# The second part of 76 split weight tiles: made by ScalarE and an adding DMA from GpSimd where VectorE subtracted

## The chip, the cores and the metric

The kernel runs on one core of one Trainium2 chip. The metric is the device time of one execution in microseconds (us). Times given as median are over three runs.

## What is computed

The reference is a network of two layers over 1024 tokens of width 1024, in float32. The first layer mixes tokens by attention in a sliding window, the second by the HGRN2 recurrence. Each mixer is followed by an MLP that squares a ReLU between two matrix products of width 4096.

```python
for layer in range(DEPTH):
    h = rmsnorm(x, mix_norm[layer])
    y = sliding_window_attention(h, ...) if layer % N_MIXERS == 0 else hgrn2_recurrence(h, ...)
    x = x + y
    h = rmsnorm(x, mlp_norm[layer])
    x = x + jnp.square(jax.nn.relu(h @ w_up[layer])) @ w_down[layer]
return rmsnorm(x, final_norm)
```

## The kernel before

**Split products.** A float32 matrix product is made of three products in the faster type float32r. Each operand is split in two parts: the first part, `hi`, is the operand rounded to float32r, and the second part, `lo`, is what is left of it. The three products are hi x hi, hi x lo and lo x hi (`mm3`, line 392), all added up in PSUM. For a weight tile of 128 x 512 this is done by `weight_split` (line 410): a cast writes `hi` into a buffer `wh`, and a subtraction writes `lo` into a buffer `wl`. There are five buffers each of `wr` (the raw tile as it is loaded), `wh` and `wl` (line 41). The cast may be given to ScalarE or VectorE; the subtraction goes to VectorE.

**Fewer products.** Large products run by a scheme of Strassen's kind. `strassen_weights` (line 590) loads four weight tiles `a[i, k]`, makes four sums of them, `s1` to `s4`, and gives up to seven tiles to be split, numbered 1 to 7. Of these, three are loaded tiles and not sums: `a[0, 0]` is number 1, `a[0, 1]` number 2 and `a[1, 1]` number 4. `done` names the tiles that are left out. `inner` brings in further tiles, of a second step of the scheme on smaller blocks; their names are pairs such as `(2, "12")`, and some of them are loaded tiles too.

Two functions call it:

- `pair` (line 711) is one of 16 steps of the first matrix product of an MLP, for m = 0 to 15. For m = 0 and 1 the tiles 1 and 2 are done already, so of the loaded ones number 4 is split. From m = 2 on, the tiles 2, 3 and 4 are left to inner products, so number 1 is split, and it is the first in the order.
- `two` (line 1282) is one of two units for each of the eight heads of HGRN, 16 units in all. In the first head the tiles 1 and 2 are done already; in the other 14 units all seven tiles are split.

A product of a tile is four times three matmuls of 128 x 128 by 128 x 512 (`product`, line 584): in each three, two use `wh` and the third uses `wl`. Inner products work on 256 columns.

**The order of the work.** The kernel doesn't issue its operations as they are written. `Schedule` (line 142) takes all of them with their costs, what they read and write and which engines may run them. It plays them through with these costs and latencies and issues them in the order that comes out, engine by engine (`order`, line 185). Each engine's queue, and SP's queue of DMAs, then runs in that order, and each instruction waits for what it needs. A buffer is given to the next tile when its last reader has finished. Operations on weights get a lead of 100 places (`LEAD`, line 136). A change of one cost or engine can therefore move operations elsewhere. Line 334 stands for nearly every instruction in the profile, because a helper records them there, so instructions are told apart by their tiles: `wr`, `wh`, `wl` as above, `p` and `q` for PSUM, `a`, `t` and `m` for the other buffers on the chip, `d` for DRAM.

Of the kernel before, what the change touches and what calls it, by code (L numbers as in the profile page):

```python
# [10 lines left out]
F32 = mybir.dt.float32  # L11
F32R = mybir.dt.float32r
I32 = mybir.dt.int32
AF = mybir.ActivationFunctionType
ALU = mybir.AluOpType
# [7 lines left out]
TH = T // NH  # L23
# [256 lines left out]
class Net:  # L280
# [126 lines left out]
        self.dma(r, src, 4 * P * TH)  # L407
        return r

    def weight_split(self, z):  # L410
        hi, lo = (self.tile(tag, BUFS[tag], (P, TH), F32R) for tag in ("wh", "wl"))
        self.copy(hi, z, TH, ("ACT", "DVE"), False)
        self.tt("any", lo, z, hi.bitcast(F32), ALU.subtract)
        return hi, lo

    def weight(self, src):

        self.s.lead = LEAD
        w = [self.weight_split(self.raw(src[:, c : c + TH])) for c in (0, TH)]
        self.s.lead = 0  # L420
        return w
# [168 lines left out]
    def strassen_weights(self, first, second, done=(), inner=()):  # L590

        self.s.lead = LEAD
        a = {(i, k): self.raw(src[:, k * TH : k * TH + TH]) for i, src in enumerate((first, second)) for k in range(2)}
        s1, s2, s3, s4 = (self.t(tag="m") for _ in range(4))
        self.tt("any", s1, a[1, 0], a[1, 1], ALU.add)  # L600
        self.tt("any", s2, s1, a[0, 0], ALU.subtract)
        self.tt("any", s3, a[0, 0], a[1, 0], ALU.subtract)
        self.tt("any", s4, a[0, 1], s2, ALU.subtract)
        order = [(1, a[0, 0]), (5, s1), (2, a[0, 1]), (6, s2), (3, s4), (7, s3), (4, a[1, 1])]
        order = [(name, z) for name, z in order if name not in done]
        own = {2: a[0, 1], 3: s4}
        for leaf, rows, names, places in inner:
            if rows:
                up, low = (z if isinstance(z, View) else own[z] if isinstance(z, int) else self.raw(z) for z in rows)
                upper, lower = self.t(tag="m"), self.t(tag="m")  # L610
                L, R = slice(0, 2 * P), slice(2 * P, TH)
                self.tt("any", upper[:, L], low[:, L], low[:, R], ALU.add, 2 * P)
                self.tt("any", upper[:, R], upper[:, L], up[:, L], ALU.subtract, 2 * P)
                self.tt("any", lower[:, L], up[:, L], low[:, L], ALU.subtract, 2 * P)
                self.tt("any", lower[:, R], up[:, R], upper[:, R], ALU.subtract, 2 * P)
                self.rows[leaf] = {"12": up, "56": upper, "73": lower, "4": low}
            for name, place in zip(names, places):
                order.insert(place, ((leaf, name), self.rows[leaf][name]))
        self.fourth = s4
        w = {name: self.weight_split(z) for name, z in order}  # L620
        self.s.lead = 0
        return w

# [1021 lines left out]
```

## Time and profile before

| | |
|---|---|
| median of three runs | 2114.9 us (2114.53 to 2116.04) |
| the profiled execution, span from the first to the last instruction | 2113.4 us; a time of its own beside the span isn't listed |
| granted TensorE clock, mean | 0.998 |
| DMA queue of SP | 225664 packets, 405.16 MB, 57.1% of 16 engines' span |
| packets of GpSimd's own DMAs | none |

In order of time the program does the attention layer (to about 300 us), the first MLP (its 16 pairs to about 620, its second product to about 920), HGRN (to about 1470, its projections in the first two thirds of it), and the second MLP (its 16 pairs from about 1480 to 1765, then its second product and the output).

The profile tells of engines by short names: PE is TensorE's matmuls, PEld its loads of weights (which overlap PE), DVE is VectorE, ACT ScalarE, POOL GpSimd, SP SyncE. The ends of matmuls are modelled, so a busy PE is not a PE at its peak. A row of a group gives the engine, the operation, out<-in by buffer names, the shape and the count, then busy us and the mean ns of one, then the idle time of the engine just before. A row of a timeline gives the start in us, the duration, the engine and the operation; in brackets, how long the engine sat idle before it and what ended that. SPq is the sequencer that issues SP's DMAs.

### The profile page before, as it was taken

The numbers are of one execution on the slowest core, as the hardware profiler recorded it, in microseconds if no ns is written. First come the engines' busy times: TensorE is split into PE (matmuls) and PEld (weight loads), VectorE is DVE, ScalarE is ACT, GpSimd is POOL, SyncE is SP. The second block draws the span as 40 slices with busy tenths as digits, with TensorE's granted clock in tenths as the row PEclk, the third lists the DMA queues.
The fourth block names the chain that finished last, engine by engine and source line by source line (L and its number), as shares of the span: only waits on it lengthen the run. The fifth ranks groups of instructions, "written<-read, shape, count | busy, mean of one in ns | idle before, by whom it ended". The sixth has DMA issues, their size and how long they took to land.

```text
span 2113.4 us, 35648 instructions
## 1 busy us (share of the span) xinstructions
PE 2090.4 (99%) x12220; PEld 1738.6 (82%) x12220; DVE 1900.2 (90%) x3922; ACT 1121.3 (53%) x2284; POOL 62.3 (3%) x121
## 2 busy tenths in 40 slices
PE   9999999999999999999999999999999999999998
PEld 7778777888888888888888888888788888888887
DVE  8889899999998989999888888888999999998995
ACT  5557777656564323556444444453765556432453
POOL 4030000000000000000000000000000000000000
PEclk9999999999999999999999999999999999999999
DMA  6212277867678967632222222566786767896632
GB/s 209 82 51 79 87 235 258 289 227 245 230 243 281 318 215 256 222 125 76 101 100 96 96 100 90 201 234 219 274 271 231 242 225 251 287 318 217 232 119 80
DMA packets 225845, 407.43 MB, mean 193 GB/s; under 512 B 25344, under 2 KB 30464, under 8 KB 225664
## 3 DMA queue, kind: packets, MB, share of 16 engines
q1 hardware_dynamic: 225664, 405.16, 57.1%
q8 instruction: 96, 1.57, 0.3%
q14 instruction: 85, 0.70, 0.1%
HBM read 321.17 MB, written 83.89 MB: 192 GB/s over the span
## 4 chain that ended last, share of the span: by engine, by line
PE 84%; DVE 8%; ACT 3%; issue 2%; DMA 1%; POOL 0%; POOLq 0%; SPq 0%; ACTq 0%; DVEq 0%
PE p L334 43%; PE q L334 41%; DVE t L334 4%; DVE a L334 2%; ACT t L334 2%; DVE m L334 1%; DVE wl L334 1%; ACT a L334 1%; DMA d<-t 1%; DMA t<-d 1%; ACT m L334 0%; DMA a<-in_x 0%; ACT wh L334 0%; DVE wh L334 0%; DMA wr<-in_wqkv 0%
## 5 line engine op out<-in xcount | busy, mean ns | idle before, releaser
L334 PE MATMUL p<-a,wh 128*128 128x512 f32 (+1 forms) x2880 | 816.1, 367 | 0.7 <-DVE t L334 0.4
L334 PE MATMUL q<-a,wh 128*128 128x512 f32 x2112 | 661.3, 394 | 1.2 <-ACT t L334 1.0
L334 PEld LDWEIGHTS p<-a,wh 128*128 128x128 f32 x2880 | 513.3, 188 | 93.9 <-DVE a L334 0.8
L334 PE MATMUL p<-a,wl 128*128 128x512 f32 (+1 forms) x1440 | 523.9, 364 | 0.1
L334 PEld LDWEIGHTS q<-a,wh 128*128 128x128 f32 x2112 | 389.0, 188 | 85.0 <-ACT t L334 1.9
L334 PE MATMUL q<-a,wl 128*128 128x512 f32 x1056 | 415.0, 393 | 1.1 <-DVE wl L334 1.1
L334 PEld LDWEIGHTS p<-a,wl 128*128 128x128 f32 x1440 | 270.7, 188 | 44.6 <-DVE wl L334 0.9
L334 DVE TENSOR_TENSOR wl<-wr,wh 128x512 fp32r<-128x512 f32 x352 | 240.6, 685 | 7.2 <-ACT wh L334 1.3
L334 DVE TENSOR_TENSOR wl<-m,wh 128x512 fp32r<-128x512 f32 x338 | 230.1, 686 | 10.3 <-ACT wh L334 0.9
L334 PEld LDWEIGHTS q<-a,wl 128*128 128x128 f32 x1056 | 198.3, 188 | 47.4 <-DVE wl L334 1.5
L334 ACT ACTIVATE t<-t 128x512 f32<-128x512 f32 x268 | 168.9, 633 | 121.7 <-DVE t L334 116.2
L334 ACT CAST wh<-wr 128x512 fp32r<-128x512 f32 x249 | 154.1, 619 | 147.9 <-PE p L334 104.0
L334 DVE TENSOR_TENSOR t<-t,t 128x512 f32<-128x512 f32 (+3 forms) x337 | 197.3, 598 | 16.9 <-DMA t<-d 10.2
L334 ACT CAST a<-t 128x512 fp32r<-128x512 f32 (+1 forms) x216 | 130.1, 611 | 146.3 <-PE q L334 83.0
L334 DVE TENSOR_TENSOR a<-t,a 128x512 fp32r<-128x512 f32 (+2 forms) x314 | 205.6, 676 | 2.0 <-ACT a L334 1.7
L334 ACT CAST wh<-m 128x512 fp32r<-128x512 f32 x231 | 143.4, 621 | 118.1 <-PE p L334 49.0
L334 ACT COPY t<-q 128x512 f32<-128x512 f32 (+2 forms) x201 | 112.2, 560 | 102.3 <-PE q L334 89.7
L334 DVE TENSOR_TENSOR m<-wr,wr 128x512 f32<-128x512 f32 (+1 forms) x188 | 120.9, 645 | 13.4 <-DMA wr<-in_down 13.0
L334 PE MATMUL p<-wh,a 128*128 128x512 f32 x384 | 127.1, 402 | 1.0 <-DVE c L334 1.0
L334 DVE TENSOR_TENSOR t<-t,p 128x256 f32<-128x256 f32 x294 | 117.6, 413 | 0.3
L334 PEld LDWEIGHTS q<-t,t 128*64 128x64 f32 (+1 forms) x2160 | 95.5, 144 | 13.9 <-issue 7.8
L334 PE MATMUL q<-t,t 128*64 128x32 f32 (+2 forms) x2160 | 105.4, 229 | 0.0
(129 smaller groups left out, 2393.7 us busy)
## 6 DMA issues: line engine op xcount, KB each, us to landing
t<-d SPq DMA_DIRECT2D x548, 256.0 KB, 4.0
d<-t SPq DMA_DIRECT2D x244, 256.0 KB, 2.8
wr<-in_down SPq DMA_DIRECT2D x224, 256.0 KB, 4.1
wr<-in_up SPq DMA_DIRECT2D x178, 256.0 KB, 3.8
wr<-in_win SPq DMA_DIRECT2D x68, 256.0 KB, 2.6
a<-d SPq DMA_DIRECT2D x60, 256.0 KB, 4.8
wr<-in_wqkv SPq DMA_DIRECT2D x48, 256.0 KB, 2.6
d<-a SPq DMA_DIRECT2D x48, 256.0 KB, 3.9
```

What stands on the lines that cost most here:

```text
L334: fn(*[place(a) for a in args], **{k: place(v) for k, v in kw.items()})
```

## The change

Where a tile to be split is one of the four that `strassen_weights` loads, and its name is a number and not a pair, the split is done another way. The cast to `wh` is bound to ScalarE. ScalarE then writes the negative of `wh` into `wl`, and a DMA that GpSimd issues adds the raw tile to `wl` where it lies. To the planner, the DMA costs 1100 ns on GpSimd and 3000 ns more until it has landed. Sums, inner tiles and every weight tile that doesn't come by way of `strassen_weights` are split as before.

```diff
-    def weight_split(self, z):
+    def weight_split(self, z, by_dma=False):
         hi, lo = (self.tile(tag, BUFS[tag], (P, TH), F32R) for tag in ("wh", "wl"))
+        if by_dma:
+            self.copy(hi, z, TH, ("ACT",), False)
+            self.act(lo, hi.bitcast(F32), AF.Copy, scale=-1.0)
+            self.add_by_dma(lo.bitcast(F32), z)
+            return hi, lo
         self.copy(hi, z, TH, ("ACT", "DVE"), False)
         self.tt("any", lo, z, hi.bitcast(F32), ALU.subtract)
         return hi, lo
+
+    def add_by_dma(self, out, in_):
+        self.op("Pool", self.nc.gpsimd.dma_start, [out], [out, in_], 1100.0, out, in_, accum_op=ALU.add, tail=3000.0)
...
-        w = {name: self.weight_split(z) for name, z in order}
+        loaded = set(a.values())
+        w = {name: self.weight_split(z, z in loaded and not isinstance(name, tuple)) for name, z in order}
```

## The prediction

> **What bounds the kernel now.** I read the page first: busy time of each engine, then the busy time by stage, then the order of instructions around the tiles that the change touches.
>
> ```profile
> span 2113.4 us, 35648 instructions
> PE 2090.4 (99%) x12220; PEld 1738.6 (82%) x12220; DVE 1900.2 (90%) x3922; ACT 1121.3 (53%) x2284; POOL 62.3 (3%) x121
> ```
>
> TensorE (PE) is busy 99% of the span and VectorE (DVE) 90%. An average over stages doesn't say which of them sets the pace where the change acts, so the next view cuts the span into stretches: length, then busy time of PE, PEld, DVE, ACT and POOL, the granted clock, the share of the DMA engines.
>
> ```profile
> 390.00:620.00 230.00, 230.00 (x1382) 204.10 (x1381) 212.95 (x450) 134.58 (x225) 0.00 (x0) 1.00 0.73 240
> 920.00:960.00 40.00, 39.64 (x179) 31.89 (x179) 35.42 (x64) 20.31 (x38) 0.00 (x0) 1.00 0.23 82
> 960.00:1060.00 100.00, 98.97 (x780) 81.39 (x779) 91.99 (x205) 48.91 (x105) 4.63 (x4) 1.00 0.27 93
> 1060.00:1370.00 310.00, 308.55 (x2601) 254.06 (x2600) 270.70 (x614) 141.96 (x309) 3.68 (x12) 1.00 0.33 113
> 1370.00:1470.00 100.00, 99.25 (x679) 81.97 (x678) 80.78 (x175) 40.90 (x82) 0.57 (x2) 1.00 0.68 225
> 1500.00:1545.00 45.00, 42.89 (x199) 34.49 (x198) 44.66 (x98) 27.12 (x52) 0.00 (x0) 1.00 0.80 275
> 1545.00:1765.00 220.00, 220.00 (x1317) 195.03 (x1317) 204.74 (x434) 130.69 (x220) 0.00 (x0) 1.00 0.73 241
> ```
>
> 390 to 620 and 1545 to 1765 are the pairs of the two MLP layers: PE is busy in all 230.00 and all 220.00 us, at a granted clock of 1.00. 920 to 1470 is HGRN: PE idles 0.36 + 1.03 + 1.45 + 0.75 = 3.59 us. 1500 to 1545 is the start of the second MLP, where DVE is busy in 44.66 of 45 us and PE idles 2.11. All that a faster VectorE can give back lies in these 3.59 + 2.11 = 5.7 us. Nothing else of VectorE's time is on the path: PE bounds the kernel.
>
> **The change part by part.** By the code, 76 tiles take the new way: one a pair in the MLP (2 layers x 16 = 32), and in HGRN one in each of the first two units and three in each of the other 14 (44).
>
> ```profile
> L334 DVE TENSOR_TENSOR wl<-wr,wh 128x512 fp32r<-128x512 f32 x352 | 240.6, 685 | 7.2 <-ACT wh L334 1.3
> L334 ACT ACTIVATE t<-t 128x512 f32<-128x512 f32 x268 | 168.9, 633 | 121.7 <-DVE t L334 116.2
> ```
>
> VectorE loses 76 x 0.685 = 52.1 us of subtractions; ScalarE gains 76 negative copies at 0.633 = 48.1 us, and the casts of these tiles that the planner used to give to VectorE (19 of the 76, by the listing of both programs; 9 other casts go the other way). VectorE had 17 us free in 390 to 620, ScalarE 95. Since PE is full there, the 52 us are hidden already and give nothing. PE's order of work in the listing stays the same but for a few neighbours swapped at the third and fourth pairs and in HGRN, so what counts is whether the second part (wl) is there when PE loads it. Here is one such tile, that of m = 8 in the first MLP (timeline: start, duration, engine, operation):
>
> ```profile
> 464.72 0.62 ACT L334 CAST wh<-wr 128x512 fp32r<-128x512 f32 x1 [0.73 <-PE p L334]
> ...
> 465.98 0.68 DVE L334 TENSOR_TENSOR wl<-wr,wh 128x512 fp32r<-128x512 f32 x1
> ...
> 466.69 0.33 SPq L334 DMA_DIRECT2D wr<-in_up  x1
> ...
> 470.40 1.30 ACT L334 ACTIVATE t<-t 128x512 f32<-128x512 f32 x2
> ...
> 471.20 0.19 PEld L334 LDWEIGHTS q<-a,wl 128*128 128x128 f32 x1
> ```
>
> The cast waits until PE frees a wh buffer and ends at 465.34. Two dependent ScalarE instructions take 1.30, so the negative copy ends 0.65 later, at 465.99. A handover costs about 0.03: the subtraction ends at 466.66, and the load that waited for it issues at 466.69. PE loads wl at 471.20. So the new DMA may take, from issue to landing, 471.20 - 465.99 - 0.06 = 5.15 us. I call that time L. The same distance at the last even pair (m = 14, second MLP), at an odd pair (m = 9; two casts in the line, the second ends at 482.20), at m = 4 of the second MLP, at m = 2 there, and at the HGRN tile with the shortest distance:
>
> ```profile
> 1733.27 0.62 ACT L334 CAST wh<-wr 128x512 fp32r<-128x512 f32 x1 [0.72 <-PE p L334]
> ...
> 1739.76 0.19 PEld L334 LDWEIGHTS q<-a,wl 128*128 128x128 f32 x1
> ```
> ```profile
> 480.86 1.34 ACT L334 CAST wh<-wr 128x512 fp32r<-128x512 f32 x2 [0.42 <-PE p L334]
> ...
> 489.43 0.19 PEld L334 LDWEIGHTS q<-a,wl 128*128 128x128 f32 x1
> ```
> ```profile
> 1548.33 0.60 ACT L334 CAST wh<-wr 128x512 fp32r<-128x512 f32 x1
> ...
> 1554.09 0.19 PEld L334 LDWEIGHTS q<-a,wl 128*128 128x128 f32 x1
> ```
> ```profile
> 1512.51 0.62 ACT L334 CAST wh<-wr 128x512 fp32r<-128x512 f32 x1
> ...
> 1519.54 0.19 PEld L334 LDWEIGHTS q<-a,wl 128*128 128x128 f32 x1
> ```
> ```profile
> 994.34 0.63 ACT L334 CAST wh<-wr 128x512 fp32r<-128x512 f32 x1
> ...
> 1005.91 0.19 PEld L334 LDWEIGHTS p<-a,wl 128*128 128x128 f32 x1
> ```
>
> Less 0.65 and 0.06 each: 5.16 for the ten even pairs from m = 6 on; 6.5 for the twelve odd ones from m = 5; 4.45 for the two of m = 4; 5.7 for m = 2 and 3 (four tiles, all put at the shortest); over 10 in HGRN, whose 44 tiles are safe, as are those of m = 0 and 1.
>
> What L will be, the trace doesn't show: no DMA is issued from GpSimd and none adds. The nearest rows are the issues in 390 to 620 (KB, median us to landing), one of quiet HGRN (1060 to 1370), the queue's share of 16 engines in 390 to 620, and the smallest regular GpSimd operation:
>
> ```profile
> q1 hardware_dynamic: 30109, 54.84, 72.2%
> ...
> wr<-in_up SPq DMA_DIRECT2D x62, 256.0 KB, 3.6
> d<-t SPq DMA_DIRECT2D x50, 256.0 KB, 3.0
> ```
> ```profile
> d<-t SPq DMA_DIRECT2D x44, 256.0 KB, 2.0
> ```
> ```profile
> L334 POOL TENSOR_SCALAR m<-c 128x4 f32<-128x4 f32 x32 | 12.8, 407 | 174.3 <-PE q L334 130.8 <-DVE a L334 18.7 <-DVE m L334 9.6
> ```
>
> A packet costs 0.722 x 16 x 230 / 30109 = 88 ns. A tile is 128 packets of 2 KB, 8 an engine, 0.7 us; the sum has to read the destination as well, so one more 0.7. Low end: as quick as a quiet store, 2.0. High end: a store's time and a load's one after the other, plus a GpSimd start, 3.0 + 3.6 + 0.4 = 7.0. I take 3.6 + 0.7 + 0.4 = 4.7, a load of this stage with a second read and a GpSimd start, because the traffic around it is the same. The Trainium skill, "DMA: Bandwidth & Descriptors", section "Anatomy of one DMA", fits DMAs issued from GpSimd by 2.0 us plus bytes over 436e3; for 256 KB that is an estimate of 2.6 us, and by it even m = 4 would not wait. No run here shows it yet.
>
> At L = 4.7 only m = 4 is late, twice 4.7 - 4.45 = 0.25: +0.5 us. One wait goes:
>
> ```profile
> 1523.70 0.62 ACT L334 CAST wh<-wr 128x512 fp32r<-128x512 f32 x1 [0.77 <-PE q L334]
> ```
> ```profile
> 1533.43 0.51 PE L334 MATMUL q<-a,wl 128*128 128x512 f32 x1 [1.08 <-DVE wl L334]
> ```
>
> At m = 3 of the second MLP the cast was done at 1524.32, but the subtraction stood in VectorE's queue and PE waited 1.08 us. By DMA the tile lands near 1524.32 + 0.65 + 0.06 + 4.7 = 1529.7, in time: -1.1 us.
>
> The DMA also holds the raw tile (wr) longer. In the first example its buffer is free at about 465.34 + 0.65 + 0.06 + 4.7 = 470.75 instead of 466.66, so SP, whose queue is in order, issues the next wr load 4.1 us later, and everything behind it waits. After an odd pair:
>
> ```profile
> 447.27 1.62 SPq L334 DMA_DIRECT2D wr<-in_up  x2
> ```
> ```profile
> 454.64 0.68 DVE L334 TENSOR_TENSOR m<-wr,wr 128x512 f32<-128x512 f32 x1
> ```
>
> The load issued at 447.27 would move about 3.3 later, to 450.6, and land at 454.2 with 3.6: still ahead of the sum that reads it at 454.64. The listing puts the neighbouring load ahead of it. If L is longer, VectorE waits first, and its sums are needed by PE some us later; I cost this at nothing, the cover being those 0.4 us and VectorE's lead. GpSimd's queue has 76 more instructions and nothing urgent behind them.
>
> Sum on the profiled execution: 2113.4 + 0.5 - 1.1 = 2112.8. Its own time isn't listed; the median of the runs is 2114.9, 1.5 above the span, and I add that: 2114.3.
>
> **The rivals.** (a) The DMA becomes what PE waits for. The delay repeats at every pair, because each cast waits for PE anew, and costs 10 x (L - 5.15) + 2 x (L - 4.45) + 4 x (L - 5.7) + 12 x (L - 6.5) - 1.1, each bracket from zero up. It passes 0.2% of the time (4.2 us, about what a measurement of this kernel can tell from no change) at L = 5.5, where it is 3.5 + 2.1 - 1.1 = 4.5. At 7.0 it is 18.5 + 5.1 + 5.2 + 6.0 - 1.1 = 33.7, so 2149; halfway, at 6.25, 11.0 + 3.6 + 2.2 - 1.1 = 15.7, so 2131. For it: the margin is 0.4 us on an operation that the trace doesn't hold, with DMA engines 73% busy. Against it: SP stands waiting for this very landing, so little new traffic starts beside it.
>
> One thing could lengthen L from VectorE's side:
>
> ```profile
> L334 DVE CAST wh<-m 128x512 fp32r<-128x512 f32 x26 | 11.1, 425 | 9.1 <-PE q L334 8.9
> ```
>
> These casts run at 425 ns where subtractions of the same size take 685. The Trainium skill, "SBUF — State Buffer", section "Who interferes with whom", says that such a fast copy locks GpSimd out of a shared port while a DMA's descriptors are to be written, and that a two-operand subtraction doesn't. By it, a DMA that meets a cast is up to 0.43 us late: L = 5.13, 2 x 0.68 - 1.1 = +0.3 us, still no measurable change.
>
> (b) Faster by more than 0.2%: the relief of VectorE and the new order empty all 5.7 us of PE's idle time in the changed stages: 2109.2. For it, DVE is full in 1500 to 1545; against it, HGRN's waits are short ones at each change of operand, and ScalarE, which serves many of them, gets more work.
>
> (c) ScalarE's added copies delay PSUM reads in HGRN. One 0.65 us in each of the 16 units makes 10.4 us, so about 2125. Against it: ScalarE is busy 141.96 of 310 us there, and in the listing no added copy stands directly ahead of the reads that PE waits for.
>
> **How the numbers follow.** Forecast (L below 5.5) 0.55; (a) 0.35, little of it past its end; (b) 0.05; (c) 0.05. The range goes from 2111, the edge of 0.2%, to 2149, the bound of (a); some 1 in 10 is left out. Faster 0.05, same 0.55, slower 0.35 + 0.05 = 0.40.
>
> **What would show it.** Right: PE busy in all of 390 to 620 again, GpSimd's DMAs landing in 4 to 5.3 us, no PE wait on wl at m = 3, and VectorE some 50 us less busy at nearly the same span. Wrong: waits of PE on a DMA of wl from wr at each pair (a), or on t in each HGRN unit (c). If VectorE's relief moved the span by more than 5.7 us, my reading of PE as the bound would be wrong.

## The result, and the profile after

| | before | changed |
|---|---|---|
| median of four runs each, on the same chip | 2114.7 us (2113.38 to 2116.04) | 2132.9 us (2129.43 to 2134.91) |
| profiled execution: span | 2113.4 us | 2131.3 us (its own time 2133.1) |

The ratio is 1.0081, 95% interval 1.0068 to 1.0094: the change costs some 17 us. The page of the changed kernel:

```profile
span 2131.3 us, 35981 instructions
PE 2097.2 (98%) x12220; PEld 1739.9 (82%) x12220; DVE 1857.3 (87%) x3844; ACT 1172.5 (55%) x2364; POOL 126.9 (6%) x197
```

VectorE has lost 42.9 us of work (1900.2 to 1857.3), ScalarE has gained 51.2, and the span, with the same 12220 matmuls, is 17.9 us longer. So work came off an engine that PE hardly waited for. The same seven stretches as in the prediction (length, busy time of PE, PEld, DVE, ACT and POOL, granted clock, DMA share, GB/s):

```profile
390.00:620.00 230.00, 227.35 (x1358) 200.46 (x1358) 202.70 (x432) 137.60 (x229) 10.35 (x12) 1.00 0.80 245
920.00:960.00 40.00, 40.00 (x182) 32.56 (x180) 35.36 (x68) 17.19 (x32) 0.88 (x1) 1.00 0.34 112
960.00:1060.00 100.00, 96.47 (x704) 78.41 (x704) 81.94 (x184) 59.81 (x121) 13.27 (x14) 0.98 0.42 113
1060.00:1370.00 310.00, 307.29 (x2636) 253.09 (x2635) 247.17 (x566) 165.36 (x351) 32.12 (x45) 1.00 0.49 133
1370.00:1470.00 100.00, 98.89 (x695) 82.05 (x694) 80.66 (x181) 41.12 (x83) 0.57 (x2) 1.00 0.73 240
1500.00:1545.00 45.00, 42.00 (x177) 33.19 (x176) 39.68 (x83) 30.75 (x58) 3.62 (x4) 0.96 0.83 257
1545.00:1765.00 220.00, 216.58 (x1276) 190.12 (x1275) 195.43 (x414) 133.83 (x224) 9.48 (x11) 0.99 0.79 249
```

PE was busy in all of 390 to 620 and 1545 to 1765; now it idles 2.65 and 3.42 us there. And the clock column, 1.00 throughout before, shows 0.98, 0.96 and 0.99 in three rows: some matmuls ran slowly. Matching the matmuls of the two traces one by one tells where the delay grows: 4.1 us in the first MLP, most of it at 375 to 425; 4.5 at 950 to 1000, where HGRN begins; 8.8 at 1525 to 1600, the first pairs of the second MLP. Elsewhere it changes by less than 1 us in all, and the last matmul ends 17.0 us later.

**PE waits for the new DMA, but not at each pair.** The DMA's rows (duration of the issue on GpSimd; then who waited, us and times; then issue to landing):

```profile
L334 POOL DMA_DIRECT2D wl<-wr x76: 859/862/1037, 338.5 to 1769.2; - x76
...
who waited for it (us, times):
  PEld q L334: 9.5, 8
  PE q L334: 6.3, 3
...
DMA to landing us min/median/max: 3.2/4.5/7.7
```

The median landing, 4.5 us, is what the prediction took (4.7). But only three tiles stopped the matmuls, for 6.3 us. The same query in five stretches, in order of time: m = 3 to 5 of the first MLP, m = 6 to 15, HGRN from 1000 us on, m = 2 to 5 of the second MLP, and m = 6 to 15:

```profile
L334 POOL DMA_DIRECT2D wl<-wr x3: 862/862/862, 369.1 to 411.2; - x3
DMA to landing us min/median/max: 5.6/6.4/7.1
```
```profile
L334 POOL DMA_DIRECT2D wl<-wr x10: 859/862/864, 431.5 to 598.1; - x10
DMA to landing us min/median/max: 4.0/4.9/6.4
```
```profile
L334 POOL DMA_DIRECT2D wl<-wr x40: 859/862/887, 1002.3 to 1358.3; - x40
DMA to landing us min/median/max: 3.2/3.4/7.6
```
```profile
L334 POOL DMA_DIRECT2D wl<-wr x4: 862/862/1009, 1523.1 to 1581.6; - x4
DMA to landing us min/median/max: 4.9/6.5/7.7
```
```profile
L334 POOL DMA_DIRECT2D wl<-wr x10: 859/862/864, 1603.6 to 1769.2; - x10
DMA to landing us min/median/max: 3.7/5.2/6.1
```

These are medians of 3.4 us in quiet HGRN, 4.9 and 5.2 in the regular pairs (m = 6 to 15), and 6.4 and 6.5 in the pairs before them. Where the DMA engines are busier it takes longer: they are busy 0.47 of the time from 1000 to 1360, 0.80 from 430 to 630, 0.87 from 335 to 430, 0.82 from 1500 to 1600; the HGRN tile of 7.6 is issued at 1358, where the share has risen to 0.86. The late tiles are m = 4 of the first MLP (landing 7.1 us, PE waits 1.80), and m = 2 (7.7, 2.50) and m = 4 (6.6, 2.02) of the second. This is m = 2 there, in the timeline (start, duration; in brackets the idle time before and what ended it):

```profile
1521.51 0.62 ACT L334 CAST wh<-wr 128x512 fp32r<-128x512 f32 x1
...
1522.17 0.64 ACT L334 ACTIVATE wl<-wh 128x512 fp32r<-128x512 f32 x1
...
1523.10 1.01 POOL L334 DMA_DIRECT2D wl<-wr  x1 [3.64 <-PE q L334]
...
1530.86 0.50 PE L334 MATMUL q<-a,wl 128*128 128x512 f32 x1 [2.50 <-DMA wl<-wr]
```

Negative copy to 1522.80, GpSimd starts 0.29 us behind it, landing at 1530.81, and the matmul has waited 2.50 us.

**After a long wait the clock is halved for a while.** Windows of the changed kernel: just behind that wait, a little later, and behind the wait of 1.80 us at 398.9:

```profile
1532.00:1535.40 3.40, 3.40 (x10) 2.67 (x9) 3.40 (x8) 1.26 (x2) 0.00 (x0) 0.52 0.89 277
1535.50:1540.00 4.50, 4.50 (x21) 3.68 (x20) 4.50 (x10) 4.32 (x8) 0.86 (x1) 0.99 0.80 279
```
```profile
399.00:403.00 4.00, 4.00 (x24) 3.57 (x25) 0.80 (x3) 1.25 (x3) 0.00 (x0) 1.00 0.71 226
```

The matmuls fall 1.5 us further behind in these 3.4 us, on top of the 2.50; behind 1.80 us nothing of the kind. The same happens behind the waits of 2.02 us at m = 4 (clock 0.50 from 1569.7 to 1573.1) and 2.14 us at the entry of HGRN, below: 1.5 and 1.7 us, so 4.7 us in all.

**At the entry of HGRN the planner has moved a tanh.** ScalarE before, at the square root of HGRN's norm (ACTIVATE sm<-sm), and after, where the same root stands at 977.62:

```profile
972.22 0.20 ACT L334 ACTIVATE sm<-sm 128x4 f32<-128x4 f32 x1 [0.29 <-DVE sm L334]
972.44 1.28 ACT L334 ACT_TABLE_LOAD   x1
973.74 1.16 ACT L334 ACTIVATE t<-t 128x512 f32<-128x512 f32 x2
```
```profile
974.38 1.28 ACT L334 ACT_TABLE_LOAD   x1
975.67 0.63 ACT L334 ACTIVATE t<-t 128x512 f32<-128x512 f32 x1
976.32 1.28 ACT L334 ACT_TABLE_LOAD   x1
977.62 0.20 ACT L334 ACTIVATE sm<-sm 128x4 f32<-128x4 f32 x1
...
978.32 1.28 ACT L334 ACT_TABLE_LOAD   x1
979.61 0.63 ACT L334 ACTIVATE t<-t 128x512 f32<-128x512 f32 x1
```

One tanh now goes ahead of the root, so three table loads of 1.28 us stand where one stood. VectorE waits for the second tanh, PE for VectorE, and the half clock follows (window of the changed kernel, clock 0.50):

```profile
980.27 0.69 DVE L334 SCALAR_TENSOR_TENSOR t<-t,t 128x512 f32<-128x512 f32 x1 [1.59 <-ACT t L334]
```
```profile
981.76 1.34 PE L334 MATMUL q<-c,c 128*128 128x128 f32 x8 [2.14 <-DVE c L334]
```
```profile
982.70:985.90 3.20, 3.20 (x10) 2.52 (x10) 3.20 (x7) 2.31 (x4) 0.00 (x0) 0.50 0.95 232
```

**Raw tiles come later.** SP's queue now stands waiting for the landing before it may load the next raw tile, and VectorE waits for those loads (waits of the changed kernel: total us, times, longest):

```profile
SPq L334 <- DMA wl<-wr: 257.2, 68, 13.3
```
```profile
DVE m L334 <- DMA wr<-in_up: 20.4, 16, 3.2
```
```profile
PE p L334 <- DVE t L334: 3.2, 5, 1.2
```

Before, the second of these was 4.3 us in 8 times, and the third 1.6 in 2. All of PE's waits together grew from 15.9 to 25.9 us; with the 4.7 us of half clock that is 14.7 of the 17.0 us by which the last matmul is later.

### The profile page after: what moved, and what is told of

The parts are those of the page before. It is cut to its first block, busy times and chain, and to the rows that moved or that the text cites. A ratio compares the mean times of both kernels' runs of the same rounds, so it can differ in the third digit from the quotient of the medians.

```text
span 2131.3 us, 35981 instructions
## 1 busy us (share of the span) xinstructions
PE 2097.2 (98%) x12220; PEld 1739.9 (82%) x12220; DVE 1857.3 (87%) x3844; ACT 1172.5 (55%) x2364; POOL 126.9 (6%) x197
## 3 DMA queue, kind: packets, MB, share of 16 engines
q8 instruction: 96, 1.57, 0.3%
## 5 line engine op out<-in xcount | busy, mean ns | idle before, releaser
L334 ACT CAST wh<-wr 128x512 fp32r<-128x512 f32 x268 | 165.7, 619 | 158.0 <-PE p L334 116.0
L334 ACT CAST a<-t 128x512 fp32r<-128x512 f32 x214 | 129.4, 613 | 140.9 <-PE q L334 75.6
L334 ACT CAST wh<-m 128x512 fp32r<-128x512 f32 x222 | 137.9, 621 | 104.0 <-PE q L334 50.7
L334 DVE TENSOR_TENSOR wl<-wr,wh 128x512 fp32r<-128x512 f32 x276 | 188.8, 686 | 5.5 <-ACT wh L334 1.3
L334 POOL DMA_DIRECT2D wl<-wr x76 | 65.9, 867 | 1075.0 <-DVE t L334 438.3
```

The lines of the kernel that those rows point to most:

```text
L334: fn(*[place(a) for a in args], **{k: place(v) for k, v in kw.items()})
```

## The experiments

**The theory**: the loss sits at a few places: the tiles of m = 2 to 5, whose DMA lands late while the DMA engines are fullest, and the entry of HGRN, where the new order of ScalarE costs two more table loads; behind both comes the half clock. **The rival**: each of the 76 tiles costs something alike, 17.9 / 76 = 0.24 us. Times are medians of 4 to 10 executions, and each ratio is to the kernel before on the same chip (2115.84, 2116.62 and 2116.20 us in the three groups of four).

**Some of the tiles.** Four kernels use the new way for a part of the tiles and VectorE for the others. `strassen_weights` gets one more argument:

```diff
-    def strassen_weights(self, first, second, done=(), inner=()):
+    def strassen_weights(self, first, second, done=(), inner=(), by_dma=False):
...
-        loaded = set(a.values())
+        loaded = set(a.values()) if by_dma else set()
```

HGRN's 44 tiles alone:

```diff
-        w = self.strassen_weights(up[m], up[m + half], (2, 3, 4) if leaves else (1, 2), inner)
+        w = self.strassen_weights(up[m], up[m + half], (2, 3, 4) if leaves else (1, 2), inner, False)
...
-        w = self.strassen_weights(*(self.io["win"][i, e] for i in which), (1, 2) if begun else ())
+        w = self.strassen_weights(*(self.io["win"][i, e] for i in which), (1, 2) if begun else (), (), True)
```

> The new split in HGRN's units alone (44 tiles); the MLP's pairs as before. Theory: the change costs 18 us in few places, and of these HGRN holds one, its entry, where the planner's new order on ScalarE loads activation tables twice more and PE waits 2.1 us and then runs at half clock for a while; that and small waits in each unit make 5 us, so about 2120, with no PE wait on a DMA of wl. Rival: every tile that goes this way costs alike, 18.2 / 76 = 0.24 us: 44 tiles make 10.5 us, about 2125.

Measured: 2120.27 us, ratio 1.0016 (1.0007 to 1.0026). In the trace the delay grows by 4.5 us at 950 to 1000, as in the changed kernel, where PE waits 2.1 us for the column c, and by 0.3 us in the rest of HGRN. In the other three kernels of this group the last arguments of the two calls are these. The 20 tiles of m = 6 to 15:

```diff
+        w = self.strassen_weights(..., inner, m > 5)
...
+        w = self.strassen_weights(..., (1, 2) if begun else (), (), False)
```

> The new split in the MLP's pairs from m = 6 on alone (20 tiles in two layers). Theory: there the DMA lands in time (4 to 6 us against 5.2 and 6.5 of room), so at most 1 to 1.5 us from late raw tiles: 2115 to 2116. Rival (every tile costs alike): 4.8 us, about 2119.5. The prediction's own sum would have the even pairs late by what the landing time exceeds 5.15.

Measured: 2118.16 us, ratio 1.0009 (0.9999 to 1.0018): just above the theory, below the rival, and its interval takes in no change. No matmul waits for a DMA of wl; PE's waits for VectorE's sums are 3.0 us, where the kernel before had 1.6. The 8 tiles of m = 2 to 5:

```diff
+        w = self.strassen_weights(..., inner, 1 < m < 6)
...
+        w = self.strassen_weights(..., (1, 2) if begun else (), (), False)
```

> The new split in the MLP's pairs m = 2 to 5 alone (8 tiles). Theory: these hold nearly all of what the MLP loses, because the DMA queues are fullest there and the DMA needs 6 to 8 us where there is room for 4.5 to 5.7; with the half clock after the two longest waits 10 to 12 us, so 2125 to 2127. Rival (every tile costs alike): 1.9 us, about 2117.

Measured: 2126.51 us, ratio 1.0039 (1.0025 to 1.0053). PE's wait for these tiles, and their landing:

```profile
PE q L334 <- DMA wl<-wr: 4.8, 2, 2.8
```
```profile
DMA to landing us min/median/max: 5.2/5.7/7.8
```

The two tiles of HGRN's first head:

```diff
+        w = self.strassen_weights(..., inner, False)
...
+        w = self.strassen_weights(..., (1, 2) if begun else (), (), e == 0)
```

> The new split in the first head of HGRN alone (2 tiles). Theory: these two tiles are enough to move the planner's order on ScalarE so that a tanh comes before and after the square root; two more table loads of 1.28 us, a PE wait of about 2 us and the half clock after it: 4 to 4.5 us, about 2119. Rival (every tile costs alike): 0.5 us, about 2115.2.

Measured: 2121.59 us, ratio 1.0023 (1.0012 to 1.0034), more than the theory's 4 to 4.5 us, which lie inside the interval (2.5 to 7.2 us). The trace has the two more table loads, and the delay grows by 4.5 us at 950 to 1000:

```profile
PE q L334 <- DVE c L334: 2.1, 1, 2.1
```
```profile
L334 ACT ACT_TABLE_LOAD x10 | 12.8, 1283 | 0.9 <-PEq L1622 0.7
```

Eight tiles cost four times as much as the 20 of the regular pairs, and two cost as much as all 44 of HGRN. The rival falls. The parts add to 0.16 + 0.09 + 0.39 = 0.64% of the 0.81%, the difference being within their intervals; the four tiles of m = 0 and 1 are in none of them.

HGRN's other 42 tiles (`e > 0` in the second call, `False` in the first):

> The 42 HGRN tiles of all heads but the first go by DMA; the two of the first head and the MLP's stay with VectorE; the order has 8 table loads. Theory (the HGRN loss is the entry alone): the 4 us at 975 to 1000 us are gone, at most +1 us is left, ratio 1.0000 to 1.0006. Rival (the DMA tiles of HGRN cost alike, whichever they are): 42/44 of the 0.16% that all 44 cost, ratio 1.0015.

Measured: 2117.09 us, ratio 1.0000 (0.9990 to 1.0010). 42 subtractions fewer on VectorE, 42 copies more on ScalarE and 42 DMAs more in the queues cost nothing, and give nothing.

**Without the DMA.** All 76 tiles, but VectorE adds:

```diff
-            self.add_by_dma(lo.bitcast(F32), z)
+            self.tt("any", lo, z, lo.bitcast(F32), ALU.add)
```

> All 76 tiles keep ScalarE's negative copy, but VectorE adds the tile into it, so no adding DMA runs and the order has 8 table loads as before. Theory (the time comes from the landing of the adding DMA at m = 2..5 and from the order at the entry of HGRN): ScalarE's 76 more instructions are hidden, 2113 to 2117 us, ratio 0.999 to 1.001. Rival (ScalarE's negative copies themselves, or their place ahead of its reads of the sums, cost the time): over 2121 us, ratio at least 1.003.

Measured: 2117.97 us, ratio 1.0005 (0.9996 to 1.0014). The upper end of the theory's band is passed by a little, its ratio is met; ScalarE's 76 copies aren't the loss. (There VectorE has its 76 operations again.)

**The root first.** The changed kernel, the first head's tanh bound to come behind the square root (`act` gets an argument `after`: tiles that the instruction is held to read as well):

```diff
+        self.root = y
...
-                self.act(u, z, AF.Tanh, scale=0.5)
+                self.act(u, z, AF.Tanh, scale=0.5, after=[self.root] if e + hf == 0 else [])
```

> The changed kernel, with one thing more: the first head's tanh is planned behind the square root, which takes the number of table loads from 10 to 8. Theory (the entry loss is two more table loads of 1.28 us, the wait on VectorE's column after them, and the half clock behind that wait): about 4 us less than the changed kernel, 2127 to 2130 us, ratio 1.0060 to 1.0068 to before. Rival (the entry loss comes from the DMA or from GpSimd there): no less than the changed kernel, 2132 to 2134 us, ratio 1.008.

Measured: 2131.15 us (2129.03 to 2140.73), ratio 1.0077 (1.0051 to 1.0103): by its time alone this decides nothing. Its profiled execution is the slowest of the four. In it the delay grows by 1.8 us at 950 to 1025 instead of 4.5, as the theory has it, and by 11.0 at 1525 to 1600, where two tiles landed after 8.0 and 8.2 us. The waits, and the second of them:

```profile
PE q L334 <- DMA wl<-wr: 10.3, 8, 3.7
```
```profile
1573.43 0.80 PE L334 MATMUL q<-a,wl 128*128 128x512 f32 x1 [3.69 <-DMA wl<-wr]
```
```profile
1574.00:1578.00 4.00, 4.00 (x11) 3.11 (x10) 0.00 (x0) 0.32 (x1) 0.00 (x0) 0.50 0.78 262
```

The matmuls around are in the same order in both kernels, and the four times of this kernel lie 11.7 us apart. So the landing at m = 2 to 5 seems to vary from execution to execution as well, with the halved clock widening what it costs; one trace a kernel can't show that.

**Second parts last.** The changed kernel, with another order in `product`:

```diff
-            self.mm3(ps, (w[0][:, c], w[1][:, c]), x[j], start and j == 0, j == HK - 1, n, **more)
+            for k in range(2):
+                self.mm(ps, w[0][:, c], x[j][k], start and j == 0 and k == 0, False, n, **more)
+        for j in range(HK):
+            c = slice(j * P, j * P + P)
+            self.mm(ps, w[1][:, c], x[j][0], False, j == HK - 1, n, **more)
```

> The changed kernel, but each product runs its eight matmuls with the first parts before its four with the second parts, so that the first second part is wanted six matmuls, about 1.4 us, later; the order at the entry of HGRN stays as in the changed kernel. Theory (the MLP's loss is the landing at m = 2..5 and the half clock behind the long waits): waits of 1.8, 2.0 and 2.5 us fall to 0.4, 0.6 and 1.1 us, none long enough to be followed by half clock, 4.2 us of waits and 3 us of half clock go, 2124 to 2127 us, ratio 1.0045 to 1.006. Rival (the late sums of VectorE and the load queue carry the loss): within 2 us of the changed kernel, 2131 to 2133 us.

Measured: 2123.05 us, ratio 1.0033 (1.0020 to 1.0047), 10 us below the changed kernel and 1 below the theory's band. The rival's 2131 us is far off. The waits for a DMA of wl are gone altogether. What is left is the entry of HGRN (3.7 us at 950 to 1000) and one wait on a sum of VectorE at 387 (1.57 us, with half clock behind it); HGRN takes back 2.4 us with the new order. The largest waits of PE:

```profile
PE p L334 <- DVE t L334: 4.6, 4, 1.6
...
PE p L334 <- ACT t L334: 3.0, 1, 3.0
```

**Both.** The last two edits together:

> The two mendings together on the changed kernel: the first head's tanh behind the square root, and the four matmuls with second parts last in each product. Theory (the two losses are apart and add up): the run with the second alone had 1.0033 and the entry of HGRN costs 0.16 to 0.23%, so 1.0010 to 1.0018, 2118.5 to 2120.5 us where the kernel before has 2116.5. Rival (the order in front of the square root is not the cause at the entry): 1.0030 to 1.0040, as without it.

Measured: 2119.57 us, ratio 1.0012 (1.0003 to 1.0021), 8 table loads; in its trace the delay doesn't grow at 950 to 1000. The entry is worth 1.0033 - 1.0012, 0.2%, and the two losses add up as the theory has it. That settles what the root-first kernel left open. Of waits for a DMA of wl, one of 1.2 us is in this trace.

**A longer landing told to the planner.** The changed kernel with 6000 ns in the planner's costs in place of 3000:

```diff
-        self.op("Pool", self.nc.gpsimd.dma_start, [out], [out, in_], 1100.0, out, in_, accum_op=ALU.add, tail=3000.0)
+        self.op("Pool", self.nc.gpsimd.dma_start, [out], [out, in_], 1100.0, out, in_, accum_op=ALU.add, tail=6000.0)
```

> The changed kernel, with the planner told 6.0 us in place of 3.0 us for the landing behind the issue; it then mixes the matmuls of another sum between those that need the late tile at m = 2 to 5. The entry of HGRN stays as in the changed kernel. Theory (the order was made for a landing that the chip doesn't keep): the waits on wl at m = 2 to 5 fall from 6.3 us to under 2 us and the half clock of the MLP goes, 2122 to 2127 us, ratio 1.003 to 1.0055. Rival (no order can hide it, since the raw tile itself comes late): within 2 us of the changed kernel, 2131 to 2134 us.

Measured: 2123.07 us, ratio 1.0028 (1.0019 to 1.0038). One number in the planner takes back 10 us: it mixes other matmuls in ahead of the late tile, and the row that had 6.3 us of waiting in the changed kernel has 0.3, though the DMA still takes up to 7.5 us to land:

```profile
L334 PE MATMUL q<-a,wl 128*128 128x512 f32 x1056 | 414.8, 394 | 0.3 <-DMA wl<-wr 0.3
```

The entry of HGRN has its 10 table loads and PE's wait of 2.2 us, but no half clock behind it in this trace: 3.0 us at 950 to 1000. The traced execution is the fastest of the ten, 4.3 us below their median, so what the others lose beyond it isn't in the trace.

**The DMA, read by nobody.** The 28 MLP tiles of m = 2 to 15 (`m > 1` in the first call, `False` in the second); the negative copy and the adding DMA go to a spare tile, and VectorE subtracts into wl as before:

```diff
             self.copy(hi, z, TH, ("ACT",), False)
-            self.act(lo, hi.bitcast(F32), AF.Copy, scale=-1.0)
-            self.add_by_dma(lo.bitcast(F32), z)
+            aside = self.t(tag="t")
+            self.act(aside, hi.bitcast(F32), AF.Copy, scale=-1.0)
+            self.add_by_dma(aside, z)
+            self.tt("any", lo, z, hi.bitcast(F32), ALU.subtract)
             return hi, lo
```

> The 28 MLP tiles of m = 2 to 15 (those of the runs with 20 and with 8 tiles together, which cost 0.09% and 0.39%): ScalarE's negative copy goes into a spare tile, GpSimd's DMA adds the raw tile to that, and nobody reads it; VectorE subtracts into wl as in the kernel before. All the traffic, all of GpSimd's issues and the longer hold on wr are there; only the wait of the matmuls for the landing isn't. Theory (what costs is PE's wait for the landing and the half clock behind it): ratio 0.9995 to 1.0015, what is left being VectorE's sums on raw tiles that come later. Rival (the traffic, GpSimd's access or the later raw tiles cost it): ratio at least 1.0035, as the two runs gave together.

Measured: 2122.24 us, ratio 1.0027 (1.0018 to 1.0037), between the two. The theory falls, as the whole interval lies above its 0.15%. The rival's 0.35% isn't reached by the measured 0.27%, but it lies inside the interval, so the rival isn't excluded. So the wait for the landing isn't all. VectorE waits longer for raw tiles from `up` (10.4 us in 13 times, against 4.3 in 8), and one place shows what that leads to. SP waits 5.2 us for an unread DMA that lands at 414.8, and issues the next raw tiles from 414.92 on. VectorE waits 3.44 us for one, a matmul waits 1.74 us for VectorE's sum, and the clock is 0.56 in the window behind it:

```profile
420.55 0.69 DVE L334 TENSOR_TENSOR m<-wr,wr 128x512 f32<-128x512 f32 x1 [3.44 <-DMA wr<-in_up]
```
```profile
422.92 0.47 PE L334 MATMUL p<-a,wh 128*128 128x256 f32 x2 [1.74 <-DVE t L334]
```
```profile
425.50:428.00 2.50, 2.50 (x9) 2.07 (x9) 2.41 (x5) 0.62 (x1) 0.00 (x0) 0.56 0.63 210
```

At 375 to 425 this trace's delay grows by 3.1 of its 4.8 us. The share can't be carried over whole to the changed kernel: here VectorE still has all its work, so less lead, and the spare tiles come out of its 18 buffers t.

**The harmless tiles together.** 62 tiles, without those of m up to 5 and of the first head (`m > 5` and `e > 0`):

> 62 of the 76 tiles by DMA: HGRN's but the first head's two, and the MLP's of m = 6 to 15; the 12 MLP tiles of m up to 5 and the two of the first head stay with VectorE. Theory (the loss lies in the tiles left out): 1.0000 + 1.0009 of the two parts, ratio 1.000 to 1.0015, and no less than before, since VectorE's 42 us freed lie under PE. Rival (the freed time of VectorE shows once the late tiles are out): under 0.998, as far as the 5.7 us of PE's idle time in these stages goes.

Measured: 2117.79 us, ratio 1.0008 (0.9999 to 1.0018). VectorE freed of 62 subtractions gives nothing back that can be measured. No kernel here beats the one before.

## Why the prediction was wrong

The time fell into the range, at 2132.9 of 2111 to 2149, and on the side that had 0.40; the forecast, 2114.3, was wrong. By its steps:

- **What bounds the kernel**: right. PE does, and the subtractions lay hidden. The 42 tiles of the later heads (1.0000) and the 62 (1.0008) show that the 5.7 us of PE's idle time don't come with VectorE's relief. The group of the subtractions lost 240.6 - 188.8 = 51.8 us, as worked out (52.1).
- **L = 4.7 for every tile**: this step failed. As a median it was good (4.5), and the margins worked out for the regular pairs held: in the changed kernel's trace none of the 20 tiles of m = 6 to 15 stopped a matmul. There was luck in it: the even ones landed in 3.7 to 5.2 us where there was room for 5.15, the odd ones in 5.2 to 6.4 where there was room for 6.5. The rows behind 4.7 were medians of 390 to 620 as a whole, and the two tiles of m = 4, with the least room of all, and that of m = 2 of the second MLP are among those that took longest: L was 7.1 and 6.6, and 7.7 at m = 2. The sum had 0.25 us each for the two of m = 4, against 1.80 and 2.02 us measured, and nothing for m = 2, against 2.50: 6.3 instead of 0.5. The margins themselves were right: with the measured landings in the prediction's own brackets these three tiles give 2.65 + 2.15 + 2.0 = 6.8 us.
- **The wait that goes** at m = 3 of the second MLP, -1.1 us: right. The tile landed in 4.9 us, and PE doesn't wait there now.
- **The raw tile held longer, costed at nothing**: failed as well. The cover of 0.4 us was gone (20.4 us of VectorE's waits for raw tiles against 4.3), and PE's waits for sums of VectorE rose. In the kernel with the unread DMA this and the traffic cost 0.27%; how much of the changed kernel's 0.81% it is stays open.
- **"PE's order of work stays the same but for a few neighbours"**: true of PE, but the order of ScalarE was looked at only for copies ahead of the reads that PE waits for. A tanh ahead of the root, with its two table loads, stands in no term of the sum and in no rival ((c) is about copies); it cost 0.2%, 4.5 us in the trace.
- **The price of a wait** was taken as the wait itself. Behind three of the four longest waits of the changed kernel (2.02, 2.14 and 2.50 us) the half clock added 1.5 to 1.7 us each. The windows of the kernel before couldn't show it, as its longest wait in these stages was 1.1 us.
- **Rival (a)** named the right mechanism, but "at every pair" was wrong: its formula, with one L for all tiles, put most of the cost on ten pairs of which none stopped a matmul. That 2132.9 lies near its middle value, 2131, is chance: 4.5 us of the loss is the table loads, which it doesn't have.

The estimate by the Trainium skill's "DMA: Bandwidth & Descriptors", section "Anatomy of one DMA", 2.6 us for such a DMA, isn't met by any of the 76: from the start of the issue the quickest took 3.2, and HGRN's median is 3.4. By the Trainium skill's "SBUF — State Buffer", section "Who interferes with whom", VectorE's fast copies could hold up the descriptors, which the prediction put at up to 0.43 us; the issues took 859 to 1037 ns, so at most 0.18 us of that shows in their durations.

## What to carry to other kernels

A transfer on the path isn't priced by the median of its stage: look at the consumer with the least room, and at what the queues do at that moment. Where a planner sets the order, give it the landing that the chip shows, and look through every engine's order for what moved (a table load, a load that waits for a buffer), not only the bound engine's. Here, work taken off an engine that the bound engine hardly waited for gave nothing, and what took its place cost time.

## What the runs showed of the hardware

- **Half clock after waits of 2 us.** In the traces of the kernels here, five waits of PE from 2.5 to 3.7 us were all followed, within 2 us, by matmuls of 512 columns at 427 ns apart instead of 232, up to 4 or 5 us behind the wait. Of fifteen waits from 1.5 to 2.2 us later than 320 us, seven were and eight weren't; of the shorter ones, none but the pair of 1.3 and 1.4 us, 0.8 us apart, at the end of every run. One wait of 1.54 to 1.56 us at 82 to 87 us stands in all fourteen kernels, and in two of them it was. The same 2.1 us at the entry of HGRN was followed by it in three kernels (the changed one, HGRN alone, its first head alone) and not in the one with the longer planned landing. The Trainium skill, "TensorE: Matmul & The Clock Gate", section "What's actually happening", tells of a window of about 3.4 us that runs freely and isn't started by the kernel. That a wait of one length goes both ways agrees with that; that a whole window of idling is needed, as its table has it, doesn't, with 2.0 us enough here, and once 1.57. The clock records of the traces tell more: before the end of the run each stretch of half clock lasts 3.41 us (one lasts 6.83), and the stretches of one trace begin whole multiples of 3.413 us apart. Cut into windows of that length from there, PE idled 1.57 to 2.86 us in the window before each stretch, and at most 1.77 us in any window that none followed. The 2.15 us that went free in the kernel with the longer planned landing lay across two windows, 1.65 and 0.50; the 2.14 us of the changed kernel lay in one.
- **An adding DMA** of 256 KB within the chip: 0.86 us of GpSimd's time for most issues, 0.29 us from the end of ScalarE's copy to its start (0.97 once), and 3.2 to 8.4 us from that start to the landing. In the changed kernel the median was 3.3 us for the 30 tiles behind whose issue the DMA engines were busy less than 0.70 of the next 5 us, 4.4 for the 23 up to 0.85, and 5.4 for the 23 above it (3.6 to 7.7).
- **A switch of table** cost 1.28 us on ScalarE in the rows above: the instruction behind starts 0.01 to 0.02 us after the load, and so does the load after the instruction before it.
